# Holding back four kinds of instruction, splitting two small square-root chains, and re-timing the output finishes in a float32 decoder layer

## The chip, the cores and the metric

The kernel runs on one core of one Trainium2 chip. The metric is the device time of one execution in microseconds (us). Engines are named as in the profile: PE (TensorE matmul), DVE (VectorE), ACT (ScalarE), POOL (GpSimd), SP (SyncE, which here only issues transfers). Each engine works through its own instructions in order.

## What is computed

One layer over a prompt of 2048 tokens and 64 sample tokens, with a model width of 2048. Everything is float32. Cut to what matters:

```python
z = rms_norm(x, pre_g)
xr, gr, u, v, gs = split(z @ w_in)                       # each 1024 wide
xc, new_buf = causal_depthwise_conv(xr, conv_buf, conv_w, conv_b)
hr, h_last = rg_lru(xc, reset, h0, w_r, b_r, w_i, b_i, lam)   # two gates, then a scan over time
br = hr * silu(gr)
v  = rms_norm(gelu(v), sgu_g)                            # the norm of v
bs = chunk_spatial_gating(gelu(u), v, w_s, b_s) * silu(gs)
out = concatenate([br, bs]) @ w_out
y  = x + rms_norm(out, post_g)                           # the norm of the output
```

## The kernel before

**Tiling.** The prompt is worked through in four quarters of 512 tokens; the first, quarter 0, also carries the 64 sample tokens. A weight piece is 128 x 1024 float32 (512 KB). It is loaded into `wraw` on SP's queue (`load_one`), ACT copies its high part to `wh` (`hi_one`, L187), and DVE subtracts that to get the low part `wl` (`lo_one`, L195). A float32 product is then three matmul passes over high and low parts. `wraw`, `wh` and `wl` have three buffers each, so that the load of a piece waits for the subtraction of the piece three before it.

**Quarter 0** is a plain product, made in jobs (xr, gr, v, gs, u, out). A scheduler orders it by priorities: an instruction may float ahead of others that were written before it, unless `later` (which is `tc.keep_in_program_order`) holds it behind everything written before it on its engine. Quarter 0 also prepares sums of weight quadrants for the later quarters. For each unit, `load_quadrants` starts four loads on POOL's queue (tiles `pB11`, `pB12`, `pB22`, `pB21`), and `make_sums` makes four additions and four stores. Units whose name begins with "c" add on DVE (L248, L250, L252, L254), the others on POOL.

**Quarters 1 to 3** use those sums in a product with seven multiplications in place of eight. Their order is written by hand in a list of steps, `steps2`; a step is the matmuls of one weight piece. For step s the code emits loads, high parts, the work in `early[s]` and `tasks[s]`, the low parts of step s+2, the matmuls of step s, and then the work in `late[s]`. `at2(s, ...)` fills those tables. In a quarter that begins at step G, the gate stage is G to G+55, the v stage begins at V = G+56, the u and gs stage at U = G+84, and the output stage at O = G+140; R2 = G+168.

**The places that the change touches.**

- `norm_v` (L926) makes 1/sqrt of the mean square of v: a sum on DVE, then `rsqrt_small` (L146): a scale-and-add on DVE (L150), a square root on ACT (L151), and five small operations on DVE (L152 to L156). It stands at U+2. `scale_v` multiplies v by the result, the first half of the heads at U+3 and the other half at U+5. `spatial_prod` (PE, tile `sp`) first reads that v at the end of step U+4.
- `out_rstd` does the same for the output of a quarter, two steps after its end.
- `norm_a("o")` and `norm_b("o")` make and broadcast the output norm of quarter 0 by matmuls (tiles `nsAo` to `nsDo`), at the end of steps 4 and 10 of `steps2`. `norm_b` goes: DVE `dgo` (L294), PE `nsCo` (L296), DVE copy (L298), DVE `dgo` (L300), PE `nsDo` (L302), DVE copy (L304).
- A finish writes one piece of the output: load the raw output from memory into `fo` (POOL's queue), scale it on DVE, add x to it by an accumulating transfer (POOL's queue), store it (POOL's queue). Quarter 0's 16 finishes run in quarter 1, in pieces of 288 KB; of quarter 1's and 2's finishes four each run in the v stage of the next quarter, in pieces of 512 KB. Their tiles come from the pool `dp` of 13 slots (`dbl`) that all working tiles share.
- `stat_sum` (ACT squares) and `z_norm` (DVE) prepare x for the next quarter; for quarter 1 they run inside quarter 0's scheduled part.

## Time and profile before

| | |
|---|---|
| Median of 3 runs | 2570.75 us (2570.57 to 2571.52) |
| The profiled execution's own time | 2568.9 us |
| Its span | 2567.1 us |
| PE busy | 2497.7 us (97% of the span) |
| DVE busy | 1748.8 us |
| ACT busy | 1391.6 us |
| POOL busy | 470.5 us |
| Mean granted TensorE clock | 0.991 of full |

Where PE is busy nearly all the time, what can be gained at unchanged work is PE's idle time, and the time in which its clock is at half. The rows below are read for those: what ended each wait of PE, and what the engine that ended it had itself been waiting for. In a row of the timeline, the bracket gives the idle time of that engine just before the row, and what ended it.

### The profile page before, as it was taken

The numbers are of one execution on the slowest core, as the hardware profiler recorded it, in microseconds if no ns is written. First come the engines' busy times: TensorE is split into PE (matmuls) and PEld (weight loads), VectorE is DVE, ScalarE is ACT, GpSimd is POOL, SyncE is SP. The second block draws the span as 40 slices with busy tenths as digits, with TensorE's granted clock in tenths as the row PEclk, the third lists the DMA queues.
The fourth block names the chain that finished last, engine by engine and source line by source line (L and its number), as shares of the span: only waits on it lengthen the run. The fifth ranks groups of instructions, "written<-read, shape, count | busy, mean of one in ns | idle before, by whom it ended". The sixth has DMA issues, their size and how long they took to land.

```text
span 2567.1 us, 41558 instructions
## 1 busy us (share of the span) xinstructions
PE 2497.7 (97%) x16710; PEld 2300.2 (90%) x16710; DVE 1748.8 (68%) x2244; ACT 1391.6 (54%) x1777; POOL 470.5 (18%) x548
## 2 busy tenths in 40 slices
PE   7989999999999999999999999999999999999997
PEld 6989789999999998799878998799878998799886
DVE  7776155545466686756888686756888687756866
ACT  5444342223324577545756677545756577645654
POOL 4331024964751201100100100100000100100000
PEclk9999999999999999999999999999999999999999
DMA  6995389985964766756776755855776755855576
GB/s 226 332 328 214 107 286 322 369 276 193 323 221 155 228 210 207 233 182 187 268 260 197 239 192 180 252 178 186 258 274 197 240 177 185 254 192 181 187 253 198
DMA packets 167649, 587.11 MB, mean 229 GB/s; under 512 B 19216, under 2 KB 19776, under 8 KB 167456
## 3 DMA queue, kind: packets, MB, share of 16 engines
q1 hardware_dynamic: 107184, 378.11, 44.5%
q0 software_dynamic: 59696, 205.30, 24.0%
q8 instruction: 130, 2.13, 0.3%
q10 hardware_dynamic: 576, 1.05, 0.1%
q14 instruction: 63, 0.52, 0.1%
HBM read 494.92 MB, written 89.47 MB: 228 GB/s over the span
## 4 chain that ended last, share of the span: by engine, by line
PE 77%; DMA 7%; DVE 7%; ACT 5%; issue 3%; POOL 1%; SPq 0%; DVEq 0%; ACTq 0%; POOLq 0%
PE gm0out L370 8%; PE gm0v L381 4%; PE gm0gs L370 4%; PE gm0u L370 4%; PE gm0gr L370 3%; DMA wraw_c_P<-P_c 2%; PE gm0xr L370 2%; DVE wl_c_B L195 1%; DMA wraw_c_B<-w_in 1%; PE g L862 1%; PE sp L559 1%; PE w2o1a L716 1%; PE w2o1d L716 1%; PE w3o0d L716 1%; PE w1o1a L716 1%
## 5 line engine op out<-in xcount | busy, mean ns | idle before, releaser
L187 ACT ACTIVATE wh_c_P<-wraw_c_P 128x1024 fp32r<-128x1024 f32 x192 | 203.0, 1059 | 255.4 <-DMA wraw_c_P<-P_c 73.8
L195 DVE TENSOR_TENSOR wl_c_P<-wraw_c_P,wh_c_P 128x1024 fp32r<-128x1024 f32 x192 | 234.3, 1221 | 105.4 <-ACT wh_c_P L187 103.2
L195 DVE TENSOR_TENSOR wl_c_B<-wraw_c_B,wh_c_B 128x1024 fp32r<-128x1024 f32 x144 | 175.4, 1221 | 86.0 <-ACT wh_c_B L187 85.9
L187 ACT ACTIVATE wh_c_B<-wraw_c_B 128x1024 fp32r<-128x1024 f32 x144 | 152.2, 1058 | 147.6 <-DMA wraw_c_B<-w_in 24.8
L187 ACT ACTIVATE wh_w_or_P<-wraw_w_or_P 128x1024 fp32r<-128x1024 f32 x96 | 101.6, 1058 | 83.9 <-DMA wraw_w_or_P<-P_w_or 27.7
L195 DVE TENSOR_TENSOR wl_w_or_P<-wraw_w_or_P,wh_w_or_P 128x1024 fp32r<-128x1024 f32 x96 | 117.4, 1223 | 40.9 <-ACT wh_w_or_P L187 40.4
L187 ACT ACTIVATE wh_w_or_B<-wraw_w_or_B 128x1024 fp32r<-128x1024 f32 x72 | 76.1, 1059 | 79.6 <-DMA wraw_w_or_B<-w_or 15.8
L370 PE MATMUL gm0out<-c0l,wh_out 128*128 128x288 f32 x512 | 110.5, 297 | 1.0 <-DVE c0l L161 0.8
L370 PE MATMUL gm0out<-c0h,wh_out 128*128 128x288 f32 x512 | 110.7, 297 | 0.0
L370 PE MATMUL gm0out<-c0h,wl_out 128*128 128x288 f32 x512 | 110.1, 296 | 0.0
L195 DVE TENSOR_TENSOR wl_w_or_B<-wraw_w_or_B,wh_w_or_B 128x1024 fp32r<-128x1024 f32 x72 | 87.9, 1221 | 30.0 <-ACT wh_w_or_B L187 29.5
L195 DVE TENSOR_TENSOR wl_out<-wraw_out,wh_out 128x1024 fp32r<-128x1024 f32 x32 | 53.0, 1657 | 54.0 <-ACT wh_out L187 53.9
L620 POOL DMA_DIRECT2D xs<-xt x24 | 12.9, 538 | 391.5 <-PE sp L559 291.9
L370 PEld LDWEIGHTS gm0out<-c0l,wh_out 128*128 128x128 f32 x512 | 82.0, 188 | 1.6 <-DVE c0l L161 1.4
L431 POOL DMA_DIRECT2D wg<-w_g x16 | 11.9, 743 | 387.9 <-ACT xch L846 128.9
L370 PEld LDWEIGHTS gm0out<-c0h,wh_out 128*128 128x128 f32 x512 | 82.0, 188 | 0.6 <-issue 0.5
L370 PEld LDWEIGHTS gm0out<-c0h,wl_out 128*128 128x128 f32 x512 | 82.2, 188 | 0.0
L187 ACT ACTIVATE wh_out<-wraw_out 128x1024 fp32r<-128x1024 f32 x32 | 33.8, 1056 | 83.4 <-PE gm0out L370 51.6
L195 DVE TENSOR_TENSOR wl_w_v_P<-wraw_w_v_P,wh_w_v_P 128x1024 fp32r<-128x1024 f32 x48 | 58.5, 1221 | 29.6 <-ACT wh_w_v_P L187 29.6
L187 ACT ACTIVATE wh_w_v_P<-wraw_w_v_P 128x1024 fp32r<-128x1024 f32 x48 | 50.0, 1054 | 48.7 <-DMA wraw_w_v_P<-P_w_v 32.7
L370 PE MATMUL gm0gr<-z0h,wl_gr 128*128 128x288 f32 x256 | 57.3, 305 | 8.3 <-DVE wl_gr L195 8.3
L370 PE MATMUL gm0xr<-z0h,wh_xr 128*128 128x288 f32 x256 | 56.6, 303 | 7.2 <-ACT wh_xr L187 5.4
(1609 smaller groups left out, 8660.9 us busy)
## 6 DMA issues: line engine op xcount, KB each, us to landing
wraw_c_P<-P_c SPq DMA_DIRECT2D x192, 512.0 KB, 4.2
wraw_c_B<-w_in SPq DMA_DIRECT2D x144, 512.0 KB, 4.3
wraw_w_or_P<-P_w_or SPq DMA_DIRECT2D x96, 512.0 KB, 4.3
wraw_w_or_B<-w_or SPq DMA_DIRECT2D x72, 512.0 KB, 3.8
wraw_w_v_P<-P_w_v SPq DMA_DIRECT2D x48, 512.0 KB, 3.6
wraw_w_v_B<-w_v SPq DMA_DIRECT2D x36, 512.0 KB, 3.5
wraw_out<-w_out SPq DMA_DIRECT2D x32, 512.0 KB, 4.5
xs<-xt POOLq DMA_DIRECT2D x24, 512.0 KB, 5.8
```

Of the source, the lines that this page charges most:

```text
L187: nc.scalar.activation(h[:, sl], raw[:, sl], AF.Copy)
L195: nc.vector.tensor_sub(l[:, sl], raw[:, sl], h[:, sl].bitcast(F32))
L370: nc.tensor.matmul(p[:, :n], w, zz[:, o:o + n], start=(k == 0 and n_pass == 0), stop=(k == KT - 1 and n_pass == 2))
L381: nc.tensor.matmul(p[:n], zz[:, c * P:c * P + n], w, start=(k == 0 and n_pass == 0), stop=(k == KT - 1 and n_pass == 2))
L431: side.dma_start(w2.rearrange("p (h c) -> p h c", h=2), a["w_g"][hp_:hp_ + 2].rearrange("h p a c -> p h (a c)"))
L559: nc.tensor.matmul(p[:, c * P:(c + 1) * P], state["vn", c, h // 4][:, vs], wst[:, h, :], start=True, stop=True)
L620: side.dma_start(x, a[f"xt{g}"][c * P:(c + 1) * P, b * W:(b + 1) * W])
L716: nc.tensor.matmul(bks[b], zz, w, start=(not cont and kk == 0 and n_pass == 0), stop=(kk == HALF - 1 and n_pass == 2), skip_group_check=True)
L862: nc.tensor.matmul(p, ww[:, ws], xx[:, i, :TP], start=n_pass == 0, stop=n_pass == 2)
```

## The change

1. **Held back by `later`**: the first addition of each sum unit on DVE; the ACT square of `stat_sum` and the first row of `z_norm`, both for quarter 1 only.
2. **Roots in two parts**: `rsqrt_small` is split into `rsqrt_begin` (scale-and-add, square root) and `rsqrt_end` (the five small operations). `norm_v` keeps the begin at U+2; `norm_v_end` stands at U+4, and the first `scale_v` moves from U+3 to U+4, behind it. `out_rstd` begins two steps after the quarter's end and ends four steps after it. `norm_a("o")` moves from step 4 to step 8, `norm_b("o")` from step 10 to step 14.
3. **Finishes**: those of quarter 0 run from 14 + 2j for j below 7 (before, 12 + 2j for j below 8) and from V+9 + 2(j-7) for the others (before, V+3 + 2(j-8)). Those of quarters 1 and 2 in the v stage scale at V+18 + 2n (before, V+21 + 3n) and load 4 steps ahead of that (before, 5). Addition and store keep their distance from the scaling.

```diff
     def rsqrt_small(ss, n, out, name):
+        rsqrt_end(out, *rsqrt_begin(ss, n, name))
+
+    def rsqrt_begin(ss, n, name):
         w = ss.shape[-1]
         s = mp.tile([P, 2, 8], F32, tag="rsm", name=f"rsm{name}")
         m, q = s[:ss.shape[0], 0, :w], s[:ss.shape[0], 1, :w]
         nc.vector.tensor_scalar(m, ss, 1.0 / n, EPS, op0=ALU.mult, op1=ALU.add)
         nc.scalar.activation(q, m, AF.Sqrt)
+        return m, q
+
+    def rsqrt_end(out, m, q):
         nc.vector.reciprocal(out, q)
...
-        eng.tensor_add(t["B11"], t["B11"], t["B12"])
+        i = eng.tensor_add(t["B11"], t["B11"], t["B12"])
+        if unit[0] == "c":
+            later(i)
...
-        nc.scalar.activation(x, x, AF.Square, accum_out=state["xss", g][:, c, b:b + 1])
+        i = nc.scalar.activation(x, x, AF.Square, accum_out=state["xss", g][:, c, b:b + 1])
+        if g == 1:
+            later(i)
...
+            if g == 1 and i == 0:
+                later(n)
...
     def norm_v(g):
         sv = mp.tile([P, 4], F32, tag="vsv", name=f"vsv{g}")
+        nc.vector.reduce_sum(sv, state["vss", g], axis=AX.X)
+        state["rvh", g] = rsqrt_begin(sv, NH * P, f"v{g}")
+
+    def norm_v_end(g):
         rv = state["rv", g] = mp.tile([P, 4], F32, tag="vrv", name=f"vrv{g}")
-        nc.vector.reduce_sum(sv, state["vss", g], axis=AX.X)
-        rsqrt_small(sv, NH * P, rv, f"v{g}")
+        rsqrt_end(rv, *state.pop(("rvh", g)))
...
-                t = 12 + 2 * j if j < 8 else V + 3 + 2 * (j - 8)
+                t = 14 + 2 * j if j < 7 else V + 9 + 2 * (j - 7)
...
-            at2(V + 16, load_gq, g - 1, 0)
+            at2(V + 13, load_gq, g - 1, 0)
             for n in range(4):
                 k = (g - 1, n % 2, n // 2)
-                t = V + 21 + 3 * n
-                at2(t - 5, finish_load, *k)
+                t = V + 18 + 2 * n
+                at2(t - 4, finish_load, *k)
...
         at2(U + 2, norm_v, g)
-        at2(U + 3, scale_v, g, 0)
+        at2(U + 4, norm_v_end, g)
+        at2(U + 4, scale_v, g, 0)
         at2(U + 5, scale_v, g, 1)
...
             at2(len(steps2) + 2, out_rstd, g)
+            at2(len(steps2) + 4, out_rstd_end, g)
...
-    late[4].append((norm_a, "o"))
-    late[10].append((norm_b, "o"))
+    late[8].append((norm_a, "o"))
+    late[14].append((norm_b, "o"))
```

How the order moves is shown at three places, all on DVE. The line numbers of the kernel after are 6 to 20 higher (L248 there is L254, L195 is L201).

In quarter 0, in the part that runs at 175 to 182 us before, DVE has first the additions of a sum unit (`pB`), then the gate work of the recurrent branch (`r`, `i`, `xc`), then the low part `wl_gr` of a weight piece. Before:

```order
L248 TENSOR_TENSOR pB11c_0_2618<-pB11c_0_2618,pB12c_0_2620 128x1024
L489 MEMSET r_2_1464 128x1
L491 TENSOR_TENSOR i_2_1475<-i_2_1475,r_2_1464 128x576
L489 MEMSET r_3_1486 128x1
L250 TENSOR_TENSOR pB12c_0_2620<-pB12c_0_2620,pB22c_0_2622 128x1024
L496 TENSOR_TENSOR i_2_1475<-i_2_1475,ah_1679 128x8
L498 SCALAR_TENSOR_TENSOR xc_2_1000<-a_2_1660,i_2_1475 128x512
L501 SCALAR_TENSOR_TENSOR xc_2_1000<-a_2_1660,i_2_1475 128x64
L500 COPY hcar<-xc_2_1000 128x1
L491 TENSOR_TENSOR i_3_1497<-i_3_1497,r_3_1486 128x576
L504 COPY nhs<-xc_2_1000 128x8
L195 TENSOR_TENSOR wl_gr_1_1764<-wraw_gr_1_1760,wh_gr_1_1762 128x1024
```

The same place of the kernel after:

```order
L497 MEMSET r_2_1464 128x1
L499 TENSOR_TENSOR i_2_1475<-i_2_1475,r_2_1464 128x576
L497 MEMSET r_3_1486 128x1
L504 TENSOR_TENSOR i_2_1475<-i_2_1475,ah_1679 128x8
L506 SCALAR_TENSOR_TENSOR xc_2_1000<-a_2_1660,i_2_1475 128x512
L509 SCALAR_TENSOR_TENSOR xc_2_1000<-a_2_1660,i_2_1475 128x64
L508 COPY hcar<-xc_2_1000 128x1
L499 TENSOR_TENSOR i_3_1497<-i_3_1497,r_3_1486 128x576
L512 COPY nhs<-xc_2_1000 128x8
L201 TENSOR_TENSOR wl_gr_1_1764<-wraw_gr_1_1760,wh_gr_1_1762 128x1024
```

The two additions that stood ahead of `wl_gr` are gone from here; this unit's additions now come 110 rows further down.

At steps U+2 to U+4 of quarter 2 the names are `vsv`, `rsmv`, `vrv` for the root of v's norm, `vn` for v, `fo` for a finish, `wl_c` for low parts. Before:

```order
L195 TENSOR_TENSOR wl_c_0_P_16544<-wraw_c_0_P_16461,wh_c_0_P_16538 128x1024
L1011 SCALAR_TENSOR_TENSOR fo_1_1_16445<-fo_1_1_16445,ors_13968,gq_0_16241 128x512 x2
L929 TENSOR_REDUCE vsv_16579<-vss_16151 128x4
L150 TENSOR_SCALAR rsmv_16582<-vsv_16579 128x4
L152 RECIPROCAL vrv_16580<-rsmv_16582 128x4
L153 TENSOR_TENSOR rsmv_16582<-vrv_16580 128x4
L154 TENSOR_TENSOR rsmv_16582<-rsmv_16582 128x4
L155 TENSOR_SCALAR rsmv_16582<-rsmv_16582 128x4
L156 TENSOR_TENSOR vrv_16580<-vrv_16580,rsmv_16582 128x4
L195 TENSOR_TENSOR wl_c_0_B_16590<-wraw_c_0_B_16479,wh_c_0_B_16572 128x1024
L935 TENSOR_SCALAR vn_0_16152<-vn_0_16152,vrv_16580 128x512 x2
L935 TENSOR_SCALAR vn_1_16405<-vn_1_16405,vrv_16580 128x512 x2
```

After:

```order
L201 TENSOR_TENSOR wl_c_0_P_16549<-wraw_c_0_P_16468,wh_c_0_P_16543 128x1024
L940 TENSOR_REDUCE vsv_16582<-vss_16151 128x4
L153 TENSOR_SCALAR rsmv_16584<-vsv_16582 128x4
L201 TENSOR_TENSOR wl_c_0_B_16587<-wraw_c_0_B_16487,wh_c_0_B_16577 128x1024
L201 TENSOR_TENSOR wl_c_0_B_16618<-wraw_c_0_B_16505,wh_c_0_B_16616 128x1024
L158 RECIPROCAL vrv_16648<-rsmv_16584 128x4
L159 TENSOR_TENSOR rsmv_16584<-vrv_16648 128x4
L160 TENSOR_TENSOR rsmv_16584<-rsmv_16584 128x4
L161 TENSOR_SCALAR rsmv_16584<-rsmv_16584 128x4
L162 TENSOR_TENSOR vrv_16648<-vrv_16648,rsmv_16584 128x4
L950 TENSOR_SCALAR vn_0_16152<-vn_0_16152,vrv_16648 128x512 x2
L950 TENSOR_SCALAR vn_1_16413<-vn_1_16413,vrv_16648 128x512 x2
```

Two low parts now stand between the two halves of the root, the finish's scaling is gone from here, and v is scaled behind the second low part instead of behind the first.

At step 10 of the first later quarter, where quarter 0's output norm is broadcast, the names are `dgo` and `rsBo` for the norm and `R1F` for sums of the activations. Before:

```order
L195 TENSOR_TENSOR wl_c_0_P_8303<-wraw_c_0_P_8172,wh_c_0_P_8293 128x1024
L690 TENSOR_TENSOR R1F_8297<-xr_6_7391,R1F_8297 128x512
L690 TENSOR_TENSOR R1F_8299<-xr_7_7393,R1F_8299 128x512
L195 TENSOR_TENSOR wl_c_0_B_8336<-wraw_c_0_B_8215,wh_c_0_B_8331 128x1024
L294 TENSOR_TENSOR dgo_8117<-ident,rsTo_8115 128x512
L298 COPY rsBo_8116<-nsCo_8364 128x512
L300 TENSOR_SCALAR dgo_8117<-ident,rsTo_8115 64x64
L304 COPY rsBo_8116<-nsDo_8368 128x64
L161 TENSOR_TENSOR wgl_0_8376<-wg_0_8301,wgh_0_8375 128x512
```

After, four steps later:

```order
L816 TENSOR_TENSOR gr_0_8156<-q1xg0d,uw1xg_8007 128x256
L201 TENSOR_TENSOR wl_c_0_P_8473<-wraw_c_0_P_8363,wh_c_0_P_8465 128x1024
L302 TENSOR_TENSOR dgo_8273<-ident,rsTo_8271 128x512
L306 COPY rsBo_8272<-nsCo_8501 128x512
L308 TENSOR_SCALAR dgo_8273<-ident,rsTo_8271 64x64
L312 COPY rsBo_8272<-nsDo_8505 128x64
L847 SCALAR_TENSOR_TENSOR xc_0_8469<-xr_0_8155,cv,xc_0_8469 128x512 x2
```

The `R1F` sums are no longer just ahead of `dgo`; the first convolution taps (`xc`) are now behind it.

## Rows read from the trace of the kernel before

**Rows 1.** Page, part 1: each engine's busy time, share of the span, instructions.

```profile
PE 2497.7 (97%) x16710; PEld 2300.2 (90%) x16710; DVE 1748.8 (68%) x2244; ACT 1391.6 (54%) x1777; POOL 470.5 (18%) x548
```

**Rows 2.** PE's waits by what ended them: engine, the waiting tile and line, what ended the wait, us in total, times, longest.

```profile
PE gm0gr L370 <- DVE wl_gr L195: 8.3, 2, 4.8
...
PE q2ug0a L702 <- DVE wl_c_B L195: 3.6, 2, 3.2
PE nsCo L296 <- DVE dgo L294: 2.5, 1, 2.5
PE w1vd L716 <- DVE wl_w_v_P L195: 2.2, 2, 1.7
PE q3ug0a L702 <- DVE wl_c_B L195: 2.2, 1, 2.2
PE q1xg1d L702 <- DVE wl_c_B L195: 2.0, 1, 2.0
...
PE w1vb L716 <- ACT wh_w_v_P L187: 1.4, 1, 1.4
```

**Rows 3.** Busy time of each engine in the stretches in which the granted clock was at half, each chosen to begin and end with it: stretch, length, PE busy (instructions), PEld, DVE, ACT, POOL, granted clock, DMA share, GB/s.

```profile
180.51:187.33 6.82, 5.74 (x24) 5.75 (x25) 6.82 (x17) 2.21 (x3) 2.73 (x6) 0.50 0.96 316
832.45:839.28 6.83, 5.40 (x17) 3.74 (x18) 3.15 (x6) 0.13 (x1) 0.00 (x0) 0.50 0.28 90
1658.48:1665.31 6.83, 5.39 (x25) 5.39 (x26) 6.79 (x13) 1.86 (x3) 0.73 (x1) 0.50 0.90 229
2242.16:2245.57 3.41, 3.41 (x18) 3.41 (x18) 3.41 (x6) 1.06 (x1) 0.42 (x1) 0.50 1.07 325
```

**Rows 4.** DVE's timeline in quarter 0, at the additions of two sum units and the low parts behind them.

```profile
123.91 1.23 DVE L248 TENSOR_TENSOR pB11c<-pB11c,pB12c 128x1024 f32<-128x1024 f32 x1 [4.28 <-DMA pB12c<-w_in]
...
133.11 1.20 DVE L195 TENSOR_TENSOR wl_gr<-wraw_gr,wh_gr 128x1024 fp32r<-128x1024 f32 x1
...
174.96 1.23 DVE L248 TENSOR_TENSOR pB11c<-pB11c,pB12c 128x1024 f32<-128x1024 f32 x1 [3.09 <-DMA pB12c<-w_in]
...
177.00 1.22 DVE L250 TENSOR_TENSOR pB12c<-pB12c,pB22c 128x1024 f32<-128x1024 f32 x1
...
180.32 1.22 DVE L195 TENSOR_TENSOR wl_gr<-wraw_gr,wh_gr 128x1024 fp32r<-128x1024 f32 x1
```

**Rows 5.** DVE's timeline at quarter 0's output norm.

```profile
830.98 1.22 DVE L195 TENSOR_TENSOR wl_c_B<-wraw_c_B,wh_c_B 128x1024 fp32r<-128x1024 f32 x1
832.11 0.68 DVE L294 TENSOR_TENSOR dgo<-ident,rsTo 128x512 f32<-128x512 f32 x1
```

**Rows 6.** Page, part 5, the high and the low part of a weight piece (busy us, mean ns of one, idle before and its releaser); and part 6, the loads of one kind of piece (count, KB, median us to landing).

```profile
L187 ACT ACTIVATE wh_c_P<-wraw_c_P 128x1024 fp32r<-128x1024 f32 x192 | 203.0, 1059 | 255.4 <-DMA wraw_c_P<-P_c 73.8
L195 DVE TENSOR_TENSOR wl_c_P<-wraw_c_P,wh_c_P 128x1024 fp32r<-128x1024 f32 x192 | 234.3, 1221 | 105.4 <-ACT wh_c_P L187 103.2
...
wraw_c_B<-w_in SPq DMA_DIRECT2D x144, 512.0 KB, 4.3
```

**Rows 7.** PE's timeline in quarter 1: the first matmuls of two steps that follow each other.

```profile
1073.79 0.40 PE L702 MATMUL q1ug0e<-R1A,wh_c_P 128*128 128x256 f32 x2
...
1076.59 0.40 PE L702 MATMUL q1ug0e<-R1A,wh_c_P 128*128 128x256 f32 x2
```

**Rows 8.** ACT's timeline in the v stage of quarter 1.

```profile
1021.92 0.60 ACT L802 ACTIVATE vn<-w1va 128x512 f32<-128x512 f32 x1 [3.20 <-DMA y<-fo]
```

**Rows 9.** DMA issues in the v stage of quarter 1, 1030 to 1050 us: weight pieces, KB each, median us to landing.

```profile
wraw_w_v_P<-P_w_v SPq DMA_DIRECT2D x5, 512.0 KB, 6.7
```

**Rows 10.** The same for 1626 to 1656 us, the end of quarter 2's v stage: x added to finishes, and weight pieces.

```profile
fo<-xt POOLq DMA_DIRECT2D x4, 512.0 KB, 9.7
wraw_c_B<-w_in SPq DMA_DIRECT2D x4, 512.0 KB, 7.9
```

**Rows 11.** ACT's timeline in the gate stage of quarter 3, where four finishes stand two steps apart.

```profile
2021.12 1.06 ACT L187 ACTIVATE wh_c_P<-wraw_c_P 128x1024 fp32r<-128x1024 f32 x1 [3.95 <-DMA wraw_c_P<-P_c]
```

**Rows 12.** DVE's timeline at the root of v's norm in quarter 2.

```profile
1657.75 0.18 DVE L152 RECIPROCAL vrv<-rsmv 128x4 f32<-128x4 f32 x1 [4.54 <-ACT rsmv L151]
...
1659.78 1.67 DVE L935 TENSOR_SCALAR vn<-vn,vrv 128x512 f32<-128x512 f32 x4
```

**Rows 13.** ACT's timeline there: the high parts for steps U+4 and U+5; the square root stands between them.

```profile
1654.66 1.06 ACT L187 ACTIVATE wh_c_B<-wraw_c_B 128x1024 fp32r<-128x1024 f32 x1 [3.03 <-DMA wraw_c_B<-w_in]
...
1657.77 1.06 ACT L187 ACTIVATE wh_c_B<-wraw_c_B 128x1024 fp32r<-128x1024 f32 x1
```

**Rows 14.** PE's timeline there: the first matmuls of step U+4, and the spatial product behind that step.

```profile
1656.26 0.51 PE L702 MATMUL q2ug0a<-R2A,wh_c_B 128*128 128x256 f32 x2 [0.74 <-ACT uw2ug L725]
...
1664.78 1.30 PE L559 MATMUL sp<-wst,vn 128*128 128x128 f32 x8
```

**Rows 15.** ACT's timeline at the same place of quarter 3: again the two high parts.

```profile
2236.51 1.06 ACT L187 ACTIVATE wh_c_B<-wraw_c_B 128x1024 fp32r<-128x1024 f32 x1
...
2240.27 1.06 ACT L187 ACTIVATE wh_c_B<-wraw_c_B 128x1024 fp32r<-128x1024 f32 x1 [0.70 <-DMA wraw_c_B<-w_in]
```

**Rows 16.** ACT's timeline at the same place of quarter 1: the high part for step U+5.

```profile
1077.28 1.05 ACT L187 ACTIVATE wh_c_B<-wraw_c_B 128x1024 fp32r<-128x1024 f32 x1
```

**Rows 17.** PE's timeline there: the spatial product.

```profile
1082.28 1.05 PE L559 MATMUL sp<-wst,vn 128*128 128x128 f32 x8
```

**Rows 18.** DVE's timeline at the root of quarter 2's output norm, early in quarter 3.

```profile
1981.53 0.18 DVE L152 RECIPROCAL ors<-rsmo 128x4 f32<-128x4 f32 x1 [2.30 <-ACT rsmo L151]
```

More of the change, by code (lines that the diff above doesn't have):

```diff
@@ L655, in z_norm @@
         for i in rows:
-            nc.vector.scalar_tensor_tensor(x[:, i, :TP], x[:, i, :TP], col(C_PRE, 2 * j + i), state["rB", g],
-                                           op0=ALU.mult, op1=ALU.mult)
+            n = nc.vector.scalar_tensor_tensor(x[:, i, :TP], x[:, i, :TP], col(C_PRE, 2 * j + i), state["rB", g],
+                                               op0=ALU.mult, op1=ALU.mult)
+            if g == 1 and i == 0:
+                later(n)
     def parts(key, j):
@@ L986, in out_rstd, with out_rstd_end @@
         sv = mp.tile([P, 4], F32, tag="osv", name=f"osv{g}")
+        nc.vector.reduce_sum(sv, state["oss", g], axis=AX.X)
+        state["orh", g] = rsqrt_begin(sv, D, f"o{g}")
+    def out_rstd_end(g):
         state["ors", g] = mp.tile([P, 4], F32, tag="ors", name=f"ors{g}")
-        nc.vector.reduce_sum(sv, state["oss", g], axis=AX.X)
-        rsqrt_small(sv, D, state["ors", g], f"o{g}")
+        rsqrt_end(state["ors", g], *state.pop(("orh", g)))
     def load_gq(g, q):
```

## The prediction

> **What bounds the kernel now.** First the page: PE is busy 2497.7 of 2567.1 us [rows 1], so at unchanged work only its 69 us of idle time and its time at half clock can be won. Next PE's waits by what ended them [rows 2]. The reader is to see that the large ones that this change can reach end with DVE: low parts in quarter 0 (8.3 us in two waits), low parts early in the u and gs stage of quarters 2 and 3 (3.2 and 2.2), the output norm of quarter 0 (2.5), and the v stage of quarter 1 (1.4 and 2.2). Then the stretches in which the granted clock was at half, 1.2 in place of 2.4 GHz [rows 3]: each begins about where one of these waits ends. Work done there takes twice its time, so a stretch costs half of PE's busy time in it: 2.9, 2.7, 2.7 and 1.7 us. Last, the timelines of DVE and ACT, for what the engine that ended a wait had itself waited for.
>
> The Trainium skill has a rule for that price (TensorE: Matmul & The Clock Gate, "HAM oscillation — how this bites in real kernels"): it charges half of the whole throttled time. By it three of the four would cost 3.4 us each; the rows show PE partly idle there, and that idle time is already counted among the waits, so I go by the rows.
>
> **The change, part by part.**
>
> *Term 1, additions held back.* In quarter 0 DVE reached an addition whose operand had not landed, stood 4.28 and 3.09 us, and only then came to `wl_gr`, at 133.11 and 180.32 [rows 4]. PE's two waits for it are the 8.3 us. With the additions of that unit gone from ahead of it, the second `wl_gr` starts 3.09 + 1.23 + 1.22 = 5.5 us earlier, against a wait of 4.8; the first starts at least 4.28 + 1.23 = 5.5 earlier, against 3.5. Both waits should go, and with them the half clock of 180.51 (2.9): 11.2. I take 11. The additions themselves are not saved; they come back later, 1.23 us each, where DVE has room on the whole (68% busy), but one may land ahead of another low part. Bounds: 4 (every second gain is given back so) and 11.2. The held squares and the row of the x norm are costed at nothing: ACT, which makes the squares, is busy 54% of the span, and nothing in rows 2 waits for them; without that cover I allow 1 us either way, inside the bounds of this term.
>
> *Term 2, quarter 0's output norm four steps later.* `dgo` runs at 832.11, right behind a low part [rows 5], because DVE is full of the transition's sums; PE waits 2.5 us for it [rows 2] and half clock follows (2.7). Four steps later DVE has got through those sums. 5.2 at best. New there: the copy of `nsCo` waits for PE, and the convolution taps and the next low part are queued behind it; a DVE that is two steps ahead can afford that. I take 4.5, bounds 1 and 5.2. The moved finishes of quarter 0 start one finish later, so their scaling still finds the norm made.
>
> *Term 3, v stage of quarter 1.* ACT stood 3.20 us for a store of a finish whose tile it was to reuse [rows 8], and the high part behind it made PE wait 1.4 and, through the low part, most of 2.2 [rows 2]: 3.6. With the finishes six steps later, that tile's predecessor is no finish any more. Against it: finishes now reach to U+4. With them in flight a weight piece takes 6.7 us to land [rows 9], not 4.3 [rows 6]. Three buffers turn over in landing + 1.06 + 1.22 [rows 6], so a step can't be shorter than (6.7 + 2.28) / 3 = 2.99 us, against PE's own 2.80 [rows 7]: 0.19 a step, 3.1 over 16 steps. Low parts are made two steps ahead, a lead of 5.6 us, which could swallow it; I take 1.3 off: +2.3, bounds -3 and +3.6.
>
> *Term 4, the root of v's norm.* In quarter 2 DVE stood 4.54 us for the square root [rows 12], with the low part for step U+4 behind it. With the root in two parts, that low part follows its high part, made at 1654.66 [rows 13]: ready at 1654.66 + 1.06 + 1.22 = 1656.9, while step U+4 begins at 1656.26 [rows 14] and needs it one matmul later. The waits of 3.2 and 2.2 go, and their half clocks (2.7 and 1.7): 9.8. But v is now scaled behind the *next* low part, and the spatial product at the end of step U+4 reads v. Quarter 2: high part 1657.77 + 1.06 [rows 13], low part 1.22, five small operations about 1.0 (an estimate from the 0.18 us of one and the gaps between them), scaling 1.67 [rows 12]: 1662.7, while PE, no longer held, arrives at 1656.9 + 2.8 = 1659.7. A new wait of 3.0, unless the pieces land earlier. Quarter 3: 2240.27 + 1.06 [rows 15] + 1.22 + 1.0 + 1.67 = 2245.2, with PE there at about 2242.3: 2.9. Quarter 1: 1077.28 + 4.95 [rows 16] = 1082.2, and PE came at 1082.28 [rows 17]: just in time, but with less lead than before. I take 2.5, 2.3 and 0.5, and half of the half clock, 2.2, as staying: 9.8 - 5.3 - 2.2 = +2.3. Bounds: -2.6 (waits of 3, 3 and 2 and all of the half clock) and +9.8.
>
> *The root of the output's norm.* DVE stood 2.30 us [rows 18], but none of PE's waits in rows 2 is there: the lead of the low parts covers it. Nothing.
>
> *Term 5, denser finishes in quarters 2 and 3.* Twelve transfers of 512 KB, before from V+16 to V+36, now run from V+14 to V+30. Where they overlap, weight pieces took 7.9 us [rows 10]; (7.9 + 2.28) / 3 = 3.39, 0.59 a step. Over 16 steps that is 9.4, less the lead of 5.6: 3.8 a quarter. In the gate stage, where finishes already stand two steps apart, ACT waited 3.95 us for a piece [rows 11]. In return the store traffic ends six steps sooner, and the gate at U+4 is freer. I take -2.5 for both, bounds -7.6 and +1.
>
> The Trainium skill has a rule that speaks against this part (DMA: Bandwidth & Descriptors, "Issuing engines are not separate DMA queues"): transfers issued by SP and by POOL run on the same 16 engines and interleave, so a second queue brings no bandwidth. The trace agrees so far as 4.3 against 7.9 us goes; with an even share at all times a piece would take 8.6, which is the last rival.
>
> **Sum.** 11 + 4.5 + 2.3 + 2.3 - 2.5 = 17.6. The profiled execution took 2568.9 us; the median of the runs is 1.85 above it. 2568.9 - 17.6 + 1.85 = 2553.
>
> **The rivals.**
>
> *A, no new waits:* pieces land early enough at U+4, and the lead holds: 11.2 + 5.2 + 3.6 + 9.8 + 1 = 30.8, or 2540. For it: finishes leave U+4 sooner. Against: the times of rows 13 and 15 are set by ACT's own order as much as by landings. 22%.
>
> *B, the wait changes its name:* the spatial product takes over all that the low part gave back, and loads lag: terms 3 to 5 at -3, -2 and -5 in sum -10, which leaves 5.5, or 2565. For it: the 3.0 and 2.9 worked out above. 17%.
>
> *C, the held additions don't free the low parts:* they come back in front of the next ones, and term 1 gives 1 at most: 7.6, or 2563. For it: twelve and more units' additions are still to be done. Against: in the order shown they are behind the low part, and 5.5 us exceed both waits. 6%.
>
> *D, slower: weights starve in the v stages.* If a piece takes 8.6 us (twice 4.3) throughout, a step needs 3.63 us, 0.83 too much; 16 steps less the lead lose 7.6 us, with half clock 2.7 more: 10.3 in each of quarters 2 and 3, and terms 3 and 4 fall to -3 and -2. 2570.75 - 15.5 + 5 + 20.6 = 2581. It decides against the change from a mean landing of about 7.65 us on: there a quarter loses 16 x 0.51 - 5.6 + 2.7 = 5.3, and 2 x 5.3 + 5 eats up terms 1 and 2. For it: 7.9 in rows 10. Against: that is the worst stretch of the stage, and the small pieces of quarter 1 gave 6.7. 8%.
>
> **How the numbers follow.** The forecast, terms near the values taken, 2546 to 2560, has 47%. Its centre is the predicted time. The range must reach to A (2540) and B (2565) and leaves out D and the outer parts of A: 2538 to 2566. A measurement of this kernel tells about 0.2%, or 5 us, from no change: faster is below 2565.6. The forecast, A, about half of B and two thirds of C lie there: 82%. The rest of B and C is within 0.2%: 10%. D is slower: 8%.
>
> **What would show it.** Term 1: PE's two waits on `wl_gr` and the half clock at 180 us are gone, and no addition on DVE waits for a transfer ahead of a low part. Term 2: no wait of over 1 us at `nsCo`. Term 3: no wait of ACT for a store ahead of v's first copy. Term 4: no wait on `wl_c_B` at step U+4; whether `sp` waits instead, and for what, tells the forecast from A and B. Term 5: the landing times of weight pieces from V+14 on: under 6.1 us (8.4 - 2.28) nothing is lost, near 8 the waits move into the v stage. The forecast is wrong if `sp` doesn't wait, or if the pieces land as early as they do without finishes.

## The result and the profile after

| | before | after |
|---|---|---|
| Median | 2570.64 us, 7 runs (2564.45 to 2575.18) | 2557.95 us, 7 runs (2550.51 to 2562.30) |
| Ratio | | 0.9945, 95% interval 0.9924 to 0.9966 |
| Profiled execution, its span | 2568.9, 2567.1 us | 2550.5, 2548.6 us |
| Mean granted clock | 0.991 | 0.996 |

The change makes the kernel 12.7 us faster by the medians (forecast 17.6; predicted 2553, range 2538 to 2566). The profiled execution of the kernel after is the fastest of its seven. It gains 18.4 us against the profile before, so its trace shows more than the change gives on the median; the second profile below (e5) is of a run 2.4 us slower than the median of its six.

PE's waits by what ended them, kernel after (columns as in rows 2):

```profile
PE sp L567 <- DVE vn L950: 2.8, 3, 0.9
PE w1vd L728 <- DVE wl_w_v_P L201: 2.2, 2, 1.7
...
PE w2o0d L728 <- DVE wl_w_or_P L201: 1.8, 1, 1.8
PE q1xg1d L714 <- DVE wl_c_B L201: 1.6, 1, 1.6
PE w3vd L728 <- DVE wl_w_v_B L201: 1.5, 2, 1.1
```

Of the waits of [rows 2], those on `wl_gr` (8.3 us), on `wl_c_B` at U+4 (3.2 and 2.2), on `nsCo` over 1 us and on `wh_w_v_P` in quarter 1 are gone. New are `sp`, 0.9 us in each of three quarters, and `w2o0d` at 1.8. The wait of 1.7 us at `w1vd` on `wl_w_v_P` is there as before. Busy time in the stretches that answer to [rows 3], kernel after:

```profile
170.00:185.00 15.00, 15.00 (x115) 15.00 (x114) 14.93 (x31) 5.91 (x8) 2.19 (x5) 1.00 0.53 174
828.00:838.00 10.00, 8.82 (x67) 7.75 (x66) 8.07 (x12) 4.06 (x6) 0.00 (x0) 1.00 0.46 153
1640.00:1650.00 10.00, 9.06 (x73) 8.57 (x73) 8.90 (x18) 4.51 (x6) 0.00 (x0) 1.00 0.52 161
2223.00:2233.00 10.00, 9.06 (x73) 8.57 (x73) 9.24 (x18) 4.28 (x6) 0.00 (x0) 1.00 0.53 161
```

The reader is to see the column before the DMA share: the clock is at full in all four. [rows 3] doesn't show every stretch at half clock of the profile before. There are three more: 10.2 us at the start, from 61 us, which every profile has; the end, where PE has no work left; and one in the gate stage of quarter 3, which no term of the forecast claimed and which is gone, too:

```profile
2023.70:2027.12 3.42, 3.42 (x17) 3.42 (x17) 3.38 (x5) 2.34 (x3) 0.00 (x0) 0.50 0.87 259
```

DVE's timeline in quarter 0, for [rows 4], kernel after:

```profile
123.50 1.23 DVE L201 TENSOR_TENSOR wl_gr<-wraw_gr,wh_gr 128x1024 fp32r<-128x1024 f32 x1
130.69 1.23 DVE L254 TENSOR_TENSOR pB11c<-pB11c,pB12c 128x1024 f32<-128x1024 f32 x1
...
170.94 1.22 DVE L201 TENSOR_TENSOR wl_gr<-wraw_gr,wh_gr 128x1024 fp32r<-128x1024 f32 x1
```

The two low parts come 9.6 and 9.4 us earlier, and the addition now starts behind the first of them, with no wait for a transfer. At the root of v's norm in quarter 2, for [rows 12 to 14], DVE's and then PE's timeline, kernel after:

```profile
1640.92 1.23 DVE L201 TENSOR_TENSOR wl_c_B<-wraw_c_B,wh_c_B 128x1024 fp32r<-128x1024 f32 x1 [1.72 <-ACT wh_c_B L193]
1642.07 0.17 DVE L158 RECIPROCAL vrv<-rsmv 128x4 f32<-128x4 f32 x1
...
1643.07 1.68 DVE L950 TENSOR_SCALAR vn<-vn,vrv 128x512 f32<-128x512 f32 x4
```

```profile
1643.61 1.17 PE L567 MATMUL sp<-wst,vn 128*128 128x128 f32 x5 [0.94 <-DVE vn L950]
```

DVE no longer stands for the root (4.54 us before). It stands 1.72 us for the second high part, v is scaled behind the low part made from that, and the spatial product waits 0.94 us for v: the wait that was forecast, at a third of its size.

Where the time was won, by stretch. Each number is how much sooner (+) or later (-) PE gets through the stretch than in the profile before, read from the starts of the same matmuls in PE's timeline. "Whole" is the kernel after, in its first profile and in e5; the others are the experiments below.

| stretch before, us | whole, 1st | whole, e5 | e1 held | e2 norm | e3 roots | e4 finishes | e6 old finishes | e9 hold 8 | e12 |
|---|---|---|---|---|---|---|---|---|---|
| quarter 0 to 259 | 11.5 | 10.7 | 10.2 | 2.1 | -2.2 | -2.3 | 9.4 | 10.7 | 9.2 |
| rest of quarter 0, to 797 | -0.9 | -3.5 | -3.3 | -0.1 | -0.6 | -0.5 | -1.9 | -2.0 | -1.0 |
| output norm of quarter 0, to 846 | 8.8 | 8.8 | -0.1 | 8.8 | -0.2 | 0.9 | 8.8 | 8.8 | 8.8 |
| gates of quarter 1, to 978 | -2.4 | -4.6 | -4.0 | -4.2 | -3.7 | 0.8 | -6.6 | -2.0 | -5.7 |
| v stage of quarter 1, to 1068 | 3.7 | 3.6 | -0.2 | -0.2 | 0.2 | 3.5 | -0.1 | 3.1 | 0.7 |
| root of v, quarter 1, to 1110 | -1.0 | -1.0 | -0.2 | 0.1 | 0.2 | -1.6 | 0.2 | -1.1 | 0.3 |
| v stage of quarter 2, 1559 to 1644 | -1.7 | -1.3 | -0.6 | -1.1 | -0.4 | -1.3 | -0.4 | -1.9 | -0.5 |
| root of v, quarter 2, to 1692 | 3.8 | 4.1 | 5.3 | 0.8 | 1.5 | 1.2 | 2.0 | 3.9 | 4.6 |
| rest of quarter 2, to 1973 | -1.4 | -3.2 | -0.1 | 0.2 | 0.7 | -1.5 | 0.4 | -1.7 | 0.2 |
| v stage of quarter 3, 2145 to 2228 | -2.5 | -2.6 | -0.3 | 0.0 | -0.8 | -2.5 | -0.1 | -2.9 | 0.0 |
| root of v, quarter 3, to 2273 | 0.9 | 0.7 | -3.6 | -0.2 | -0.7 | -0.9 | -0.6 | 0.5 | 3.5 |
| all | 18.4 | 9.0 | 2.4 | 2.8 | -5.9 | -5.6 | 10.7 | 14.0 | 21.4 |

The matmuls of the output norm move from the third row into the fourth, so these two are read together. Some 2 us in the first row differ from run to run at the start-up (e2 to e4 changed nothing there). Rows that stay within 2 us of nothing in most columns are left out, and so the rows don't add up to the last.

A stretch that an edit doesn't touch can differ by 4 to 5 us between two profiles. e1 leaves the root of v as it was and has +5.3 and -3.6 there: its waits on `wl_c_B` are 1.3 and 3.2 us in place of 3.2 and 2.2. The two rows "root of v" of quarters 2 and 3 are steadier as a sum: 0.3 to 1.7 with the root in one part (e1, e2, e4), 0.8 and 1.4 with the root split and the old finishes (e3, e6), 4.4 to 4.8 with the whole change (both profiles, e9), 8.1 in e12.

### The profile page after: what moved, and what is told of

Its sections match the earlier page's. It is cut to its first block, busy times and chain, and to the rows that moved or that the text cites. A ratio compares the mean times of both kernels' runs of the same rounds, so it can differ in the third digit from the quotient of the medians.

```text
span 2548.6 us, 41550 instructions
## 1 busy us (share of the span) xinstructions
PE 2490.2 (98%) x16710; PEld 2291.3 (90%) x16710; DVE 1757.9 (69%) x2244; ACT 1391.2 (55%) x1777; POOL 468.0 (18%) x548
## 4 chain that ended last, share of the span: by engine, by line
PE 79%; ACT 6%; DVE 5%; DMA 5%; issue 3%; POOL 0%; SPq 0%; DVEq 0%; ACTq 0%; POOLq 0%
PE gm0out L378 8%; PE gm0v L389 4%; PE gm0gr L378 4%; PE gm0gs L378 4%; PE gm0u L378 4%; PE gm0xr L378 3%; DMA wraw_c_P<-P_c 1%; PE g L874 1%; PE sp L567 1%; DVE wl_c_B L201 1%; PE w3o0d L728 1%; PE w2o1d L728 1%; PE w2o1a L728 1%; PE w1o1d L728 1%; PE w1o1a L728 1%
## 5 line engine op out<-in xcount | busy, mean ns | idle before, releaser
L201 DVE TENSOR_TENSOR wl_c_P<-wraw_c_P,wh_c_P 128x1024 fp32r<-128x1024 f32 x192 | 233.9, 1221 | 98.9 <-ACT wh_c_P L193 98.7
L201 DVE TENSOR_TENSOR wl_c_B<-wraw_c_B,wh_c_B 128x1024 fp32r<-128x1024 f32 x144 | 175.7, 1221 | 105.6 <-ACT wh_c_B L193 105.5
L201 DVE TENSOR_TENSOR wl_w_or_P<-wraw_w_or_P,wh_w_or_P 128x1024 fp32r<-128x1024 f32 x96 | 117.4, 1223 | 41.2 <-ACT wh_w_or_P L193 40.7
L201 DVE TENSOR_TENSOR wl_w_or_B<-wraw_w_or_B,wh_w_or_B 128x1024 fp32r<-128x1024 f32 x72 | 88.0, 1222 | 28.4 <-ACT wh_w_or_B L193 28.1
L201 DVE TENSOR_TENSOR wl_out<-wraw_out,wh_out 128x1024 fp32r<-128x1024 f32 x32 | 46.8, 1462 | 45.0 <-ACT wh_out L193 45.0
L201 DVE TENSOR_TENSOR wl_w_v_P<-wraw_w_v_P,wh_w_v_P 128x1024 fp32r<-128x1024 f32 x48 | 58.5, 1221 | 26.0 <-ACT wh_w_v_P L193 25.8
L389 PE MATMUL gm0v<-wh_v,z0l 128*128 128x512 f32 (+1 forms) x160 | 63.2, 396 | 0.0
```

What stands on the lines that cost most here:

```text
L201: nc.vector.tensor_sub(l[:, sl], raw[:, sl], h[:, sl].bitcast(F32))
L389: nc.tensor.matmul(p[:n], zz[:, c * P:c * P + n], w, start=(k == 0 and n_pass == 0), stop=(k == KT - 1 and n_pass == 2))
```

## The experiments

All times are medians with the runs of before on the same chip beside them: 2571.04 us for e1 to e4, 2568.21 for e5 to e8, 2568.98 for e9 to e12. Between these three groups the ratio, with its 95% interval, is to be compared.

### e1: only the instructions held back

```diff
 # on the kernel before
+        if unit[0] == "c":
+            later(i)           # first addition of a sum unit; and the squares and x-norm rows of quarter 1
```

> Only the instructions held back (part 1); roots, output norm and finishes as before. If the sums' additions were what held up wl_gr (term 1): both waits of PE on wl_gr (8.3 us) and the half clock at 180 us are gone, 10 to 12 us faster than before, all of it won by 187 us of the span, and nothing else moves. If the additions come back in front of other low parts (rival C): the waits on wl_gr go, but others of the same size appear in quarter 0, and the gain is under 4 us.

2563.17 us, ratio 0.9974 (0.9961 to 0.9987). Both waits on `wl_gr` are gone and 10.2 us are won by 259 us, but 3.3 us are lost again in the rest of quarter 0, in a wait of 2.5 us of `sp`, at 580 us, that the kernel before doesn't have. Rival C was right that something comes back, and wrong on where: not another low part waits (see e5 and e9). The squares and the row of the x norm are held in e1, too. That the additions are what counted is read from DVE's order; they were not held alone.

### e2: only the output norm four steps later

```diff
 # on the kernel before
-    late[4].append((norm_a, "o"))
-    late[10].append((norm_b, "o"))
+    late[8].append((norm_a, "o"))
+    late[14].append((norm_b, "o"))
```

> Only norm_a and norm_b of quarter 0's output norm four steps later. If DVE's sums at the transition held up dgo (term 2): the wait of 2.5 us on nsCo and the half clock behind it go, 4 to 6 us faster. If that gain rests on the held additions, which in the full change also free DVE ahead of the transition: 1.5 us at most, with a wait on nsCo left.

2564.68 us, ratio 0.9977 (0.9959 to 0.9996): 6.4 us faster. The third and fourth rows of the table together give 4.6 us. A wait of 0.8 us is left at `nsCo`, without half clock. The gain doesn't rest on the held additions.

### e3: only the roots in two parts

The edit is `rsqrt_begin`, `rsqrt_end`, `norm_v_end` and `out_rstd_end` as in the change's diff, with nothing else of it.

> Only the two roots in two parts (norm_v and out_rstd), finishes as before. If the wait mostly changes its name (term 4): the waits on wl_c_B at step U+4 of quarters 2 and 3 go, sp waits 2 to 3 us in each in their place, net gain 0 to 4 us. If the freer DVE settles it alone: sp waits under 1 us, 8 to 10 us faster. If what held the root was the finishes' traffic at U to U+4 all along: waits on both, no gain.

2568.69 us, ratio 0.9999 (0.9983 to 1.0014): nothing that can be measured. PE's waits, e3:

```profile
PE sp L565 <- DVE vn L944: 3.2, 2, 1.7
```

The waits on `wl_c_B` are down to 0.3 us and `sp` waits 1.5 and 1.7 us in quarters 2 and 3: the wait changed its name, at over half of its size.

### e4: only the finishes moved

```diff
 # on the kernel before
-                t = 12 + 2 * j if j < 8 else V + 3 + 2 * (j - 8)
+                t = 14 + 2 * j if j < 7 else V + 9 + 2 * (j - 7)
...
-                t = V + 21 + 3 * n
-                at2(t - 5, finish_load, *k)
+                t = V + 18 + 2 * n
+                at2(t - 4, finish_load, *k)
```

> Only the finishes moved, roots as before. If terms 3 and 5 hold: the wait of ACT for a store in the v stage of quarter 1 goes (2 to 3.5 us won there), 1 to 4 us are lost in the v stages of quarters 2 and 3, within 3 us of before on the whole. If the clear U+4 is what the change is worth there: the waits on wl_c_B at U+4 of quarters 2 and 3 shrink by 2 us or more each even with the root in one part, 5 us or more faster. If weights starve (rival D): slower by 5 us or more, with landings near 8 us from V+14 to U+2.

2572.23 us, ratio 1.0011 (0.9997 to 1.0024). The v stage of quarter 1 wins 3.5 us, and the waits at U+4 of quarters 2 and 3 stay, at 2.3 and 2.0 us. But the finishes of quarter 0 now reach to U+4 there, and with the root in one part step U+4 of quarter 1 waits as those of quarters 2 and 3 did before. PE's timeline, e4:

```profile
1078.81 0.38 PE L702 MATMUL q1ug0a<-R1A,wl_c_B 128*128 128x256 f32 x1 [1.97 <-DVE wl_c_B L195]
```

### e5: the whole change again

> The whole change once more, as the measure for the three beside it on the same chip. By the profile of the first run, 13 to 18 us faster than before (2553 to 2558 where before takes 2571); sp waits 0.9 us in each of quarters 1 to 3.

2557.49 us, ratio 0.9958 (0.9943 to 0.9974), profiled execution 2559.9 us. This run has the wait of e1 at 580 us. PE's and ACT's timeline, e5:

```profile
582.33 1.16 PE L567 MATMUL sp<-wst,vn 128*128 128x128 f32 x8 [2.76 <-DVE s L573]
```

```profile
570.14 0.69 ACT L166 ACTIVATE c0h<-cb 128x576 fp32r<-128x576 f32 x1 [3.81 <-DMA cb<-cat]
```

ACT stands for `cb`, the concatenated branches that are read back for the last product; DVE's low parts of them follow, and `u` and `s`, which `sp` needs, are behind those on DVE. DMA issues from 550 to 575 us, e5:

```profile
cb<-cat POOLq DMA_DIRECT2D x8, 288.0 KB, 6.9
wraw_out<-w_out SPq DMA_DIRECT2D x3, 512.0 KB, 6.1
P_w_or<-pB11w_or POOLq DMA_DIRECT2D x1, 512.0 KB, 6.4
P_w_or<-pB12w_or POOLq DMA_DIRECT2D x1, 512.0 KB, 3.1
P_w_or<-pB22w_or POOLq DMA_DIRECT2D x1, 512.0 KB, 3.2
P_w_or<-pB21w_or POOLq DMA_DIRECT2D x1, 512.0 KB, 3.0
```

Four stores of a sum unit stand right ahead of `cb` on POOL's queue. They do so in the first profile, too, and there PE doesn't wait: `cb` is issued 2 us earlier and lands sooner. DMA issues from 550 to 575 us, first profile:

```profile
cb<-cat POOLq DMA_DIRECT2D x8, 288.0 KB, 5.2
```

So the stores alone don't make the wait; it is between nothing and 2.8 us in the seven profiles that hold all the units.

The two profiles of one and the same program differ by 9.4 us. Clock and span of the first and of the second:

```profile
core 0: 2548.6 us, clock 0.996
```

```profile
core 0: 2558.0 us, clock 0.992
```

Page, part 1, of the first and of the second:

```profile
PE 2490.2 (98%) x16710; PEld 2291.3 (90%) x16710; DVE 1757.9 (69%) x2244; ACT 1391.2 (55%) x1777; POOL 468.0 (18%) x548
```

```profile
PE 2497.1 (98%) x16710; PEld 2297.7 (90%) x16710; DVE 1747.6 (68%) x2244; ACT 1389.4 (54%) x1777; POOL 468.8 (18%) x548
```

6.9 of the 9.4 us are in PE's busy time, where a lower clock shows; the other 2.5 are idle time, about the wait at 580 us. So most of the difference is the clock. In the second run it fell to half after five waits. Busy time in these stretches, e5:

```profile
583.95:587.36 3.41, 3.41 (x15) 3.41 (x16) 0.10 (x1) 0.68 (x1) 2.10 (x4) 0.50 0.95 312
836.53:839.95 3.42, 3.42 (x18) 3.42 (x17) 3.38 (x5) 0.00 (x0) 0.00 (x0) 0.50 0.06 23
877.49:880.90 3.41, 3.41 (x19) 3.41 (x18) 3.41 (x6) 0.00 (x0) 0.25 (x1) 0.50 1.01 235
1017.44:1020.85 3.41, 3.41 (x9) 2.64 (x9) 3.34 (x7) 0.00 (x0) 0.16 (x1) 0.50 1.01 242
1857.12:1860.53 3.41, 3.41 (x10) 2.64 (x9) 3.41 (x5) 1.32 (x2) 0.00 (x0) 0.50 0.98 324
```

Four of the five waits ahead of these are in the first run too: 0.94 us in both at `nsDo`, 1.55 and 1.91 at `q1xg1d`, 1.68 in both at `w1vd`, 1.77 and 2.01 at `w2o0d`. There the clock stayed at full.

### e6: the whole change with the finishes where they were

The edit is part 3 of the diff, backwards.

> The whole change with the finishes left where they were (part 3 undone). If part 3 is worth nothing alone but clears U+4 for the split root (the two work together): 3 to 6 us slower than the whole change, with sp waiting 1.5 us or more in quarters 2 and 3, as it does with the roots alone, and the waits for a store back in quarter 1 (over 3 us in its gate and v stages). If the denser finishes cost what they give (terms 3 and 5 cancel): within 2 us of the whole change.

2557.24 us, ratio 0.9950 (0.9933 to 0.9968): the same as the whole change. Part 3 is worth nothing on the whole, and the table shows two halves that cancel. The old finishes lose in quarter 1 (2 to 4 us in the gates, 3.7 in the v stage) and at the roots of v in quarters 2 and 3 (1.5 to 2 each). They save 1.2 at the root of v in quarter 1, about 1 and 2.4 in the v stages of quarters 2 and 3, and 1.8 to 3.6 in the rest of quarter 2 (see e10).

Why the gates of quarter 1 gain from part 3, which I had costed at nothing, shows in ACT's timeline at the gates' second group: e1, with the old finishes, and the kernel after.

```profile
874.40 1.26 ACT L874 ACTIVATE i<-g,cv 128x512 f32<-128x512 f32 x2 [5.16 <-DMA y<-fo]
```

```profile
860.21 1.27 ACT L880 ACTIVATE i<-g,cv 128x512 f32<-128x512 f32 x2 [2.71 <-DMA y<-fo]
```

The gate's tile takes over the slot of a finish and ACT waits for that finish's store, 5.2 us and 2.7. PE waits for it at `q1xg1d`: 4.1 us in e1, e3, e6 and e12, 2.7 in e2, 2.0 in the profile before, 1.0 to 1.9 with the finishes moved. ACT's own wait there is 3.2 to 6.1 us in the six profiles with the old finishes and 1.9 to 3.1 in the eight others; in the profile before and in e6 it is put down to PE and not to the store.

### e7: second part of v's root at U+3

```diff
 # on the kernel after
-        at2(U + 4, norm_v_end, g)
-        at2(U + 4, scale_v, g, 0)
+        at2(U + 3, norm_v_end, g)
+        at2(U + 3, scale_v, g, 0)
```

> The whole change, but the second part of the root and the first scaling of v at U+3, ahead of the low part for step U+5 and not behind it. If sp waits because v is scaled behind that low part: the 0.9 us at sp go in all three quarters, and the low part comes just in time for step U+5: 1 to 3 us faster than the whole change. If the square root arrives no sooner than that low part's high part (ACT makes both, in order): DVE stands for the root again and step U+5 waits, 0 to 3 us slower.

2553.50 us, ratio 0.9936 (0.9918 to 0.9954): 4 us less than e5 by the medians, with intervals that overlap. No wait of `sp` on `vn` is left in any quarter. DVE's and then PE's timeline in quarter 2, e7:

```profile
1641.85 1.22 DVE L201 TENSOR_TENSOR wl_c_B<-wraw_c_B,wh_c_B 128x1024 fp32r<-128x1024 f32 x1 [0.58 <-ACT wh_c_B L193]
1643.85 0.18 DVE L158 RECIPROCAL vrv<-rsmv 128x4 f32<-128x4 f32 x1 [0.78 <-ACT rsmv L154]
...
1644.87 1.67 DVE L950 TENSOR_SCALAR vn<-vn,vrv 128x512 f32<-128x512 f32 x4
```

```profile
1646.39 1.05 PE L567 MATMUL sp<-wst,vn 128*128 128x128 f32 x8
```

One low part between the halves is enough: DVE stands 0.78 us for the root, and PE doesn't wait.

### e8: finishes three steps apart, and earlier

```diff
 # on the kernel after
-                t = V + 18 + 2 * n
+                t = V + 15 + 3 * n
```

> The whole change, but the finishes of quarters 1 and 2 in the v stage at V+15+3n, three steps apart (loads V+11 to V+20, last store V+30 as before). If the density of transfers starves the weights (term 5): landings of weight pieces in that stage fall from 7 to 8 us towards 6, the waits in the v stages of quarters 2 and 3 (1.4 and 2.5 us lost in the first profile) shrink by half, 1 to 3 us faster. If what counts is only when they end: the same within 1 us.

2558.44 us, ratio 0.9962 (0.9950 to 0.9974): the same. In the v stages of quarters 2 and 3 it loses 4.4 and 5.3 us, at least twice as much as two steps apart (1.3 to 2.6), and at the root of v it wins 5.3 and 1.3. Fewer transfers at once do let a piece land somewhat sooner. DMA issues in the second half of quarter 2's v stage, at the kernel after and at e8 (whose stretch lies 5 us earlier):

```profile
wraw_w_v_B<-w_v SPq DMA_DIRECT2D x4, 512.0 KB, 7.6
fo<-xt POOLq DMA_DIRECT2D x3, 512.0 KB, 10.4
y<-fo POOLq DMA_DIRECT2D x3, 512.0 KB, 11.9
```

```profile
wraw_w_v_B<-w_v SPq DMA_DIRECT2D x4, 512.0 KB, 6.9
wraw_w_v_P<-P_w_v SPq DMA_DIRECT2D x3, 512.0 KB, 6.1
fo<-xt POOLq DMA_DIRECT2D x3, 512.0 KB, 8.8
y<-fo POOLq DMA_DIRECT2D x3, 512.0 KB, 10.5
```

My expectation that the density decides fell. Why e8 loses more in the v stages is open: pieces that take over 6.1 us are not more there (7 in each of the two stages, against 8 at the kernel after).

### e9: only the first eight units held back

```diff
 # on the kernel after
-        if unit[0] == "c":
+        if unit[0] == "c" and units.index(unit) < 8:
```

> The whole change, but only the first eight sum units of kind c are held back; the later ones float as before. If the held additions of the late units push the sums of the w_or units into the loads of the concatenated branches (cb), and with that make sp wait 1 to 2.8 us at 580 us: that wait is gone, the 10 us won by 187 us stay whole, and the run is 1 to 4 us faster than the whole change. If that wait comes from PE simply being 10 us earlier against a transfer pace that no order changes: it stays, same within 1 us.

2554.56 us, ratio 0.9941 (0.9923 to 0.9960): 3 us less than e5, with intervals that overlap. The wait at 580 us is gone. DMA issues from 550 to 575 us, e9:

```profile
cb<-cat POOLq DMA_DIRECT2D x8, 288.0 KB, 4.4
wraw_out<-w_out SPq DMA_DIRECT2D x4, 512.0 KB, 3.4
```

No store of sums is left beside `cb`, and it lands in 4.4 in place of 6.9 us. It is also issued 9 us earlier. POOL's timeline, e5 and e9, the last store of sums and `cb`:

```profile
563.89 0.57 POOL L251 DMA_DIRECT2D P_w_or<-pB21w_or  x1 [0.30 <-POOL pB21w_or L262]
564.46 2.14 POOL L351 DMA_DIRECT2D cb<-cat  x4
```

```profile
548.07 0.57 POOL L251 DMA_DIRECT2D P_w_or<-pB21w_or  x1 [0.57 <-POOL pB21w_or L262]
...
555.41 2.14 POOL L351 DMA_DIRECT2D cb<-cat  x4
```

In e5 POOL comes to `cb` straight from the sums; in e9 it has been done with them for 7 us. How much of the wait is the later issue and how much the slower landing was not separated. None of the three profiles that hold eight units (e9, e11, e12) has the wait, and six of the seven that hold all have it. A wait of 1.3 us at 254 us, which the whole change doesn't have, takes part of it back.

### e10 to e12: together, with the root of the x norm in two parts

```diff
 # on the kernel after, with the edit of e7
             at2(O + 17, stat_rstd, g + 1)
+            at2(O + 19, stat_rstd_end, g + 1)     # second part of this root, too
```

e11 adds the edit of e9, and e12 that of e6 as well.

> The whole change with the second part of v's root at U+3, and the root of the x norm (stat_rstd, quarters 2 and 3) in two parts as well, O+17 and O+19. If the 1.7 to 2.0 us that PE waits for wl_w_or_P in quarter 2's output stage are DVE standing for that root: they go, 1 to 3 us faster than with the root of v at U+3 alone (2553.5). If they come from the late landing of that weight piece beside the loads of x: the wait stays.

> All three together: root of v at U+3, root of the x norm in two parts, first eight units held. If each of them removes a wait of its own, they add up: 2546 to 2550 where before takes 2570.

> The same with the finishes left where they were before. If part 3 only trades one wait for another: within 2 us of the one beside it. If the later finishes need the free U+4 that part 3 gives, now that v's root is read a step earlier: 2 to 5 us slower, with DVE standing for the root at U+3.

e10: 2551.16 us, ratio 0.9921 (0.9902 to 0.9941). The wait of `w2o0d` on `wl_w_or_P`, 1.7 to 2.0 us in the kernel after and e7, is gone. What it was shows in DVE's timeline, kernel after, and in ACT's: DVE stands for the root of the x norm, unsplit, with the low part behind it, and ACT comes late to the square root because it waits for a weight piece ahead of it.

```profile
1846.71 0.18 DVE L158 RECIPROCAL xrt<-rsmx 128x4 f32<-128x4 f32 x1 [2.75 <-ACT rsmx L154]
```

```profile
1844.10 1.06 ACT L193 ACTIVATE wh_w_or_P<-wraw_w_or_P 128x1024 fp32r<-128x1024 f32 x1 [2.96 <-DMA wraw_w_or_P<-P_w_or]
```

With the old finishes the same root, unsplit, holds DVE for 0.6 to 0.9 us and PE doesn't wait. DVE's timeline, e6:

```profile
1855.12 0.18 DVE L158 RECIPROCAL xrt<-rsmx 128x4 f32<-128x4 f32 x1 [0.83 <-ACT rsmx L154]
```

Of the profiles with this root in one part, all six with the finishes moved have the wait (0.6 to 2.0 us, 1.5 in e4, which changes nothing else), and none of the five with the old finishes. In e8 and e9, with the two smallest, DVE stands under 0.5 us for the root, so there the root is not all of it. Either way it is a cost of part 3, and part of what the rest of quarter 2 loses in the table. By what way the moved finishes delay that weight piece was not followed.

e11: 2550.65 us, ratio 0.9919 (0.9897 to 0.9941). e12, with the old finishes: 2549.10 us, ratio 0.9918 (0.9898 to 0.9938). The three can't be told apart, so my expectation that e9's edit adds to e10 isn't borne out. All are faster than the kernel before; their intervals lie below that of e5, though they overlap that of the first measurement of the kernel after (0.9924 to 0.9966). In e12 the roots of v gain 4.6 and 3.5 us and the v stages of quarters 2 and 3 lose 0.5 and nothing, though the gates of quarter 1 lose 5.7. A version with only quarter 0's finishes moved might take the good half of each; it was not tried.

## Why it came out so, by the prediction's steps

**Term 1 (forecast 11): mechanism right, size off.** The additions were what held `wl_gr`: 9.2 to 11.5 us are won by 259 us in every kernel that holds them back. Left out was the far end of the chain. Holding the additions of all units delays the sums made after them on POOL, and `cb` is issued behind their last stores; `sp` waits 1.0 to 2.8 us in six of seven profiles, with half clock in one. The rest of quarter 0 gives 0.9 to 3.5 us back; the first profile had escaped the wait. e9 shows this by taking the cause away, the late issue and the stores together. The cover "DVE has room on the whole" was true of DVE and said nothing of the queue behind the sums.

**Term 2 (4.5): right.** 4.6 us in e2, where the wait of `q1xg1d` in the same stretch was 0.6 us longer than before.

**Term 3 (2.3): mechanism right, one wait misread.** +3.6 in the v stage of quarter 1, and the wait of ACT for a store is gone. The forecast put the wait of 1.7 us at `w1vd`, most of its 2.2, down to that store; it is there unchanged in both profiles of the kernel after. What went are `w1vb`'s 1.4 and two smaller waits of 0.8 and 0.5; the rest of the 3.6 has no single wait behind it, so the agreement with 3.6 is partly luck. That the finishes then reach to U+4 cost 1.0 at the root of v there, against the 1.3 taken off here and the 0.5 under term 4.

**Term 4 (2.3): right in kind, and nearer to rival A than thought.** `sp` took over the wait, at 0.9 us in place of 2.5 and 2.3; the two roots gain 4.7 and 4.8 in sum, less 1.0 in quarter 1. The times of the two high parts, which I took over from the rows of before, were earlier against PE's arrival, since part 3 clears U+4: without it `sp` waits 1.5 to 2.4 (e3, e6). What remains is the order that I named, v behind the next low part; e7 takes it away and the wait goes.

**Term 5 (-2.5): right in sign, larger, and not by the sum that was made for it.** -1.3 to -1.7 and -2.5 in the two v stages, -4 in sum, against -0.4 and -0.1 with the old finishes. The price was worked out from landings of 7.9 over 16 steps. 7.6 and 8.0 were measured, but for four pieces each; in each of the two stages eight pieces took over 6.1 us, 7.4 on the mean. By the forecast's sum eight such steps cost 8 x ((7.4 + 2.28) / 3 - 2.80) = 3.4 us, and a lead of 5.6 would cover them. It did not; why the lead covered less is open. Rival D needed 8.6 throughout the stage.

**Edits costed at nothing.** The output's root: nothing is seen of it in PE's waits; it was not tried alone. The moved finishes in quarter 1's gate stage: wrong, 2 to 4 us won against e6. I had looked for the finishes' effect in their transfers and in the v stage's tiles, and not in the tiles of the gates, which come from the same pool. And at a root that the forecast doesn't have, that of the x norm, the same part 3 makes PE wait 1.8 us for `w2o0d` in the first profile and 2.0 in e5.

**The half clock.** The forecast took 2.9, 2.7 and 2.2 us for half clock, 7.8 of its 17.6, as if each long wait brought it and each one saved took it away. The kernel after has it in none of the places in its first run and in five others in its second. PE's idle time (the span less PE busy) is 69.4 us in the profile before, 58.4 in the first profile and 60.9 in e5. So the first profile gains 11.0 us of idle and 7.5 of busy time, e5 8.5 and 0.6, where the forecast had 9.8 for waits and 7.8 for the clock. In sum the waits came out near the forecast, and what the clock gives back depends on the run. Over all runs the mean granted clock rose from 0.991 to 0.994, so some of it is gained on the median, too. The 5 us between forecast and median are of that size; how they divide between clock and waits was not measured.

So the forecast was right in its sign, its range and, `w1vd` apart, the mechanisms of its terms. Against it stand a chain that wasn't followed to its end (term 1), the wait at the root of the x norm and the clock, for it what the gates gave. That errors of both signs nearly cancel is in part luck.

## What to carry to other kernels

When instructions are held back, follow what comes after them on every queue to its last transfer, not only to the engine that has room; a delay of some us can surface 400 us later beside a load that PE needs. A root that crosses from one engine to another and back wants its second half behind about as much other work as the answer takes: one low part sufficed here, two moved the wait to the consumer. In a pool that all stages share, moving a store moves the wait of whichever tile gets that slot next, in any stage. And one profile against one other holds the luck of both: read a gain from stretches that an edit left alone as well, to see how far they move by themselves.
